# Turning the input with VectorE in blocks of 32 and loading the input projection's weights in four pieces each

## The chip, the cores and the metric

The kernel runs on one core of a Trainium2 chip. Its time is the device time of one execution in microseconds. Three runs before the change took 1353.6, 1354.23 and 1354.41 us (median 1354.23). A profile is one further execution with every engine's instructions recorded. Five engines matter: TensorE (PE; its weight loads are shown as PEld), VectorE (DVE), ScalarE (ACT), GpSimd (POOL) and SyncE (SP), which here only issues transfers. ACT and POOL issue transfers as well.

## The reference, cut to what matters

One step of an encoder layer for two groups of rows that share the weights: 256 new frames of a prompt and 32 frames of a running stream, 288 rows in all, 2048 features each, all in float32.

```
xn   = rmsnorm(x, norm_mix_pre)
proj = xn @ w_in        # 2048 x 5664: [u_pool 1024 | z 2048 | xBC 2560 | dt 32]
pool = trailing-mean pooling mixer on u_pool
ssd  = Mamba-2 mixer on xBC, dt, gated by z   (conv, exact chunked scan, norm)
x    = x + rmsnorm(concat[pool, ssd] @ w_out, norm_mix_post)
up   = rmsnorm(x, norm_ffn_pre) @ w_up        # 2048 x 11264
f    = (silu(conv(gate)) * conv(val)) @ w_down
x    = x + rmsnorm(f, norm_ffn_post)
```

The outputs are the new x of both groups and the new states (pooling rows, two convolution histories, the scan's state).

## The kernel before, in words

**Layout.** Activations are kept transposed: the 128 partitions hold features and the 288 rows lie along the free side. 2048 features are 16 column tiles (KD). A product has 128x128 weights as the stationary operand and 128x288 activations as the moving one, and accumulates over the 16 tiles of features in a PSUM tile `acc` (five buffers).

**Precision.** Each operand is split into a high part, written by ScalarE as float32r, and the rest, subtracted by VectorE. A product is then three matmuls (`mm3`: high x high, high x rest, rest x high). Weights arrive as `raw` (four buffers of up to 1 MB), `split_w` makes `whi` on ScalarE (L146) and `wlo` on VectorE (L147), each with four buffers. The activations' split is `split_from` (L120, L121), which also multiplies by the norm's gain, a value per partition. The row factor of the norm, `rstd`, is applied to the products when VectorE takes them out of PSUM (`conv_in`, `gate_in`, `pool_in`).

**The opening.** `input_tiles` loads x with its rows on the partitions, a chunk of columns at a time. For every column tile TensorE transposes the two prompt blocks and the sample block into PSUM (L299, L300, L301), `split_from` reads PSUM and makes `xn`, and VectorE copies the tile to `xT` (L304), which ScalarE's queue stores to `xT_d` in memory for the residual sum later. `project` with `first_in` as a hook multiplies the columns of B, C and dt (256, 256 and 32 wide) chunk by chunk: 2, 2, 4, 4 and 4 column tiles, each with three weight loads. The narrow dt columns go through `split_narrow`, which puts high part and rest side by side, so that two matmuls do (L185, L186). Ahead of the last chunk `parameters` transposes the small parameters: `columns` three times (L281) and six transposes of `pf` (L325). ScalarE squares whole rows of x with an accumulated sum (L348, L349); from these sums come `rs` and, by six matmuls against the identity (L355), `rstd` on all partitions. It is 16 x (4 x 3 + 2) = 224 matmuls.

**After it.** `project` runs over groups of 256 columns, each with two loads of 1 MB (K16: eight tiles of features in each) and 96 matmuls: eight groups of x for the scan, eight of z, four of u. Between them stands the scan's work. VectorE turns finished 128x288 tiles in blocks of 32 (`blocks_out`, L206, one staging tile `blocks`), SP stores the four strips to memory (L209, `xs_d`), and SP loads them back with rows on the partitions (`xk`, L535 and L536), beside `gb` (L510) and `h0` (L514). VectorE is in every step of this: weight splits, convolution, evacuation, turns. At the start of the output projection `xT` is loaded back from `xT_d` (L887).

**Order.** Each engine and each issuing queue works through its instructions in order. The order is laid out ahead of time by a planner, from priorities and its own estimate of durations; `tc.high_priority` moves instructions forward, `tc.issue_after` puts one behind another on its engine, and `tc.keep_in_program_order` keeps marked instructions of an engine in the order of the source. A load waits on its queue until its buffer is free, and what stands behind it on that queue waits too.

Of the kernel before, what the change touches and what calls it, by code (L numbers as in the profile page):

```python
# [41 lines left out]
TAIL = NT - P  # L42


@with_exitstack
def body(
# [79 lines left out]
    ahead = [0]  # L126

    def fetch_w(view, kb, nk, c0, nc_):
# [22 lines left out]
    def split_narrow(raw, kb, nk, nc_, after):  # L151

        both = xin.tile([P, nk, 2, nc_], F32R, tag="both", bufs=2, name="both")
        with ExitStack() as order:
            order.enter_context(tc.high_priority(offset=ahead[0]))
            for ins in after:
                order.enter_context(tc.issue_after(ins.ins))
            act.activation(both[:, :, 0, :], raw, AF.Copy)
            dve.tensor_tensor(both[:, :, 1, :], raw, both[:, :, 0, :].bitcast(F32), op=ALU.subtract)
        return [(kb + k, both[:, k, :, :].rearrange("p r c -> p (r c)")) for k in range(nk)]  # L160

    def mm3(out, wh, wl, a, start, stop):
        pe.matmul(out, wh, a[:, 0, :], start=start, stop=False)  # L163
        pe.matmul(out, wh, a[:, 1, :], start=False, stop=False)  # L164
        pe.matmul(out, wl, a[:, 0, :], start=False, stop=stop)  # L165

    def project(view, groups, acts, ksplit, before=None, done=None, spare=(), hold=(), behind=None):
# [7 lines left out]
        for i, (kb, n) in enumerate(ksplit):  # L175
# [5 lines left out]
            for raw, (c0, w) in zip(raws, groups):  # L181
                if w < P:
                    for k, both in split_narrow(raw, kb, n, w, after or ()):
                        o = accs[m0][: 2 * w, :]
                        pe.matmul(o, both, acts[k][:, 0, :], start=k == k_first, stop=False)  # L185
                        pe.matmul(o, both, acts[k][:, 1, :], start=False, stop=k == k_last)  # L186
                    continue
                parts = split_w(raw, kb, n, w, ((after or ()) if m0 else ()) + (hold if i else ()))
# [24 lines left out]

    ident = const.tile([P, P], F32, name="ident")
    make_identity(nc, ident)
    ones = const.tile([P, P], F32, name="ones")
    pool.memset(ones, 1.0)
# [7 lines left out]
    tc.keep_in_program_order(act.activation(warm, eps_t, AF.Copy))  # L225
# [22 lines left out]
    start = ExitStack()  # L248
    xin = start.enter_context(tc.tile_pool(name="xin", bufs=1))

    g0_in = xin.tile([KD, P], F32, name="g0_in")
    act.dma_start(out=g0_in, in_=rows(norm_mix_pre))
# [5 lines left out]
    xt = xin.tile([P, 2, D_MODEL], F32, name="xt")  # L258
    xs_ = xin.tile([NS, D_MODEL], F32, name="xs_")
    xpv = x_prompt.rearrange("o (b p) d -> p (o b) d", p=P)  # L260
# [17 lines left out]
    def columns(src, n, name):  # L278
        o = const.tile([P, n], F32, name=name)
        p_ = aux([P, n], "pt")  # L280
        pe.transpose(p_, src, ident[:n, :n])  # L281
        dve.tensor_copy(o, p_)
        return o

    g_mix_pre = columns(g0_in, KD, "g0")


    xn = []
    xT = xin.tile([P, KD, NT], F32, name="xT")
    xT_d = dram.tile([P, KD, NT], F32, name="xT_d")  # L290

    def input_tiles(kb, n):
        c = slice(kb * P, (kb + n) * P)
        sp.dma_start(out=xt[:, :, c], in_=xpv[:, :, c])
        sp.dma_start(out=xs_[:, c], in_=x_sample[0][:, c])
        for t in range(kb, kb + n):
            p_ = aux([P, NT], "pt")
            c = slice(t * P, (t + 1) * P)
            pe.transpose(p_[:, 0:P], xt[:, 0, c], ident)  # L299
            pe.transpose(p_[:, P:NP_], xt[:, 1, c], ident)  # L300
            pe.transpose(p_[:, NP_:NT], xs_[:, c], ident[:NS, :NS])  # L301
# [5 lines left out]
        return last  # L307

    def parameters():
        pb = columns(pb_in, 108, "pb")  # L310
        g_mix_post = pb[:, 60:76]
        g_ffn_pre = pb[:, 76:92]
        g_ffn_post = pb[:, 92:108]
        pa = columns(pa_in, 124, "pa")
        pah = const.tile([P, 100], F32, name="pah")
        act.activation(pah, pa[:, 0:100], AF.Copy, scale=0.5)
        p_scale = pa[:, 100:108]
        g_ssd = const.tile([P, NX], F32, name="g_ssd")
        act.activation(g_ssd, pa[:, 108:124], AF.Copy, scale=0.5)
        pc = columns(pc_in, 120, "pc")  # L320
        pf = const.tile([P, 6, NF * 2], F32, name="pf")
        for i in range(0, 6, 3):
            p_ = aux([P, 3, NF * 2], "ptf")
            for j in range(3):
                pe.transpose(p_[:, j, :], pf_in[:, i + j, :], ident[: NF * 2, : NF * 2])  # L325
            dve.tensor_copy(pf[:, i : i + 3, :], p_)
        return pb, pah, g_mix_post, g_ffn_pre, g_ffn_post, pa, p_scale, g_ssd, pc, pf

    prm = []

    def first_in(kb, n):
        if kb == 12:
            prm.extend(parameters())
        return input_tiles(kb, n)

    win = w_in.rearrange("o (k p) c -> p (o k) c", p=P)
    O_Z, O_X = D_POOL, D_POOL + D_SSD
    O_B, O_C, O_DT = O_X + D_SSD, O_X + D_SSD + 256, O_X + CONV
    first = project(
        win, [(O_B, 256), (O_C, 256), (O_DT, HEADS)], xn, [(0, 2), (2, 2), (4, 4), (8, 4), (12, 4)], first_in  # L340
    )

    ahead[0] = 200
    ssum = xin.tile([P, 3], F32, name="ssum")
    pool.memset(ssum, 1.0)
    junk = xin.tile([P, D_MODEL], F32, name="junk")
    for b in range(2):
        act.activation(junk, xt[:, b, :], AF.Square, accum_out=ssum[:, b : b + 1])  # L348
    act.activation(junk[:NS, :], xs_, AF.Square, accum_out=ssum[:NS, 2:3])  # L349
    rs = xin.tile([P, 3], F32, name="rs")  # L350
    act.activation(rs, ssum, AF.Sqrt, bias=eps_t, scale=1.0 / D_MODEL)
    dve.reciprocal(rs, rs)
    p_ = aux([P, NT], "prs")
    for b, (o, n) in enumerate(BLK):
        pe.matmul(  # L355
            p_[:, o : o + n], rs[:n, b : b + 1].broadcast_to([n, P]), ident[:n, :n], start=True, stop=True
        )
    rstd = const.tile([P, NT], F32, tag="spread", bufs=3, name="rstd")
    dve.tensor_copy(rstd, p_)

    pb, pah, g_mix_post, g_ffn_pre, g_ffn_post, pa, p_scale, g_ssd, pc, pf = prm
    start.close()


# [857 lines left out]
```

## Time and profile before

| what | before |
|---|---|
| median of three runs | 1354.23 us |
| the profiled execution, its own time | 1354.27 us |
| span of its instructions | 1352.6 us |
| TensorE busy | 1340.1 us, 99% |
| VectorE busy | 886.6 us, 66% |
| ScalarE busy | 669.5 us, 50% |
| DMA engines, share on the SP queue | 59.0% |
| granted TensorE clock | 0.999 |
| moved in all | 252.13 MB, mean 186 GB/s |

How to read it: "busy" counts the time in which an engine has an instruction in work; matmuls overlap, so the starts of two matmuls lie closer together than each one's duration (0.29 us). A line such as L163 is a line of the kernel's source. An arrow "out<-in" names the tile written and the tiles read. "x40" is a count. "Idle before" is the engine's pause ahead of an instruction and what ended it. The DMA share is the mean busy share of the core's 16 DMA engines; since packets overlap a little it can go over 1. "To landing" is the time from a transfer's issue to its completion.

### The profile page before, as it was taken

To read this page: it belongs to the slowest core of one execution; us is meant where nothing else is said; L and a number is where in the kernel's file an instruction comes from. 1 tells how busy PE (TensorE), PEld (TensorE's weight loads), DVE (VectorE), ACT (ScalarE), POOL (GpSimd) and SP (SyncE) were. 2 spreads that over 40 slices of the span, in tenths; PEclk is the share of its full clock that TensorE was granted. 3 is DMA by queue.
4 is the path that set the end of the run, shared out by engine and by line. 5 is a ranking of instruction groups with operands and counts; after the bars stand their busy time and mean duration, and the time that the engine had idled before them with its cause. 6 is when DMAs were issued, how large, how long until landed. Compare 5 with 4: busy or idle time off the path is not lost.

```text
span 1352.6 us, 25723 instructions
## 1 busy us (share of the span) xinstructions
PE 1340.1 (99%) x10199; PEld 1327.7 (98%) x10199; DVE 886.6 (66%) x1519; ACT 669.5 (50%) x1003; POOL 233.2 (17%) x394
## 2 busy tenths in 40 slices
PE   8999999999999999999999999999999999999997
PEld 7999999999999999999999999999999999999997
DVE  6898988779644479977676644335666666664454
ACT  6557767446534455645444433334444444454443
POOL 3132112222223320211121100001111111101110
PEclk9999999999999999999999999999999999999999
DMA  8869985464756546876545545554554554576663
GB/s 269 250 192 280 257 249 167 154 221 151 243 179 201 159 132 191 239 196 182 183 156 163 173 144 169 172 179 156 175 168 156 175 169 156 170 232 181 191 182 94
DMA packets 300135, 252.13 MB, mean 186 GB/s; under 512 B 75728, under 2 KB 293050, under 8 KB 299886
## 3 DMA queue, kind: packets, MB, share of 16 engines
q1 hardware_dynamic: 296942, 243.46, 59.0%
q0 software_dynamic: 2320, 4.65, 1.2%
q10 hardware_dynamic: 752, 2.37, 0.5%
q8 instruction: 80, 1.31, 0.4%
q14 instruction: 41, 0.34, 0.1%
HBM read 236.13 MB, written 14.31 MB: 185 GB/s over the span
## 4 chain that ended last, share of the span: by engine, by line
PE 99%; DVE 0%; DMA 0%; ACT 0%; issue 0%; DVEq 0%
PE acc L163 31%; PE acc L165 31%; PE acc L164 31%; PE pst L852 1%; PE py L562 1%; PE acc L1128 1%; PE acc_x L164 0%; PE acc_x L163 0%; PE acc_x L165 0%; PE py L564 0%; DMA xt<-in_x_prompt 0%; PE pt L299 0%; PE acc L1129 0%; PE pt L301 0%; DVE wlo L147 0%; PE acc L186 0%
## 5 line engine op out<-in xcount | busy, mean ns | idle before, releaser
L147 DVE TENSOR_TENSOR wlo<-raw,whi 128x1024 fp32r<-128x1024 f32 (+1 forms) x416 | 493.3, 1188 | 347.9 <-ACT whi L146 346.6
L146 ACT ACTIVATE whi<-raw 128x1024 fp32r<-128x1024 f32 (+1 forms) x416 | 426.6, 1028 | 498.0 <-PE acc L164 421.0
L163 PE MATMUL acc<-hn,whi 128*128 128x288 f32 x1376 | 404.1, 295 | 0.0
L164 PE MATMUL acc<-hn,whi 128*128 128x288 f32 x1376 | 403.6, 294 | 0.3 <-DVE hn L911 0.3
L165 PE MATMUL acc<-hn,wlo 128*128 128x288 f32 x1376 | 403.1, 294 | 0.0
L164 PEld LDWEIGHTS acc<-hn,whi 128*128 128x128 f32 x1376 | 259.7, 189 | 0.7 <-DVE hn L911 0.7
L165 PEld LDWEIGHTS acc<-hn,wlo 128*128 128x128 f32 x1376 | 259.6, 189 | 0.0
L163 PEld LDWEIGHTS acc<-hn,whi 128*128 128x128 f32 x1376 | 257.2, 187 | 0.1
L163 PE MATMUL acc<-xn,whi 128*128 128x288 f32 x704 | 209.3, 299 | 0.0
L164 PE MATMUL acc<-xn,whi 128*128 128x288 f32 x704 | 208.0, 296 | 0.0
L165 PE MATMUL acc<-xn,wlo 128*128 128x288 f32 x704 | 207.2, 296 | 0.0
L163 PE MATMUL acc<-fa,whi 128*128 128x288 f32 x682 | 201.9, 296 | 0.0
L164 PE MATMUL acc<-fa,whi 128*128 128x288 f32 x682 | 201.9, 296 | 0.0
L165 PE MATMUL acc<-fa,wlo 128*128 128x288 f32 x682 | 201.5, 295 | 0.0
L164 PEld LDWEIGHTS acc<-xn,whi 128*128 128x128 f32 x704 | 133.6, 190 | 0.3
L165 PEld LDWEIGHTS acc<-xn,wlo 128*128 128x128 f32 x704 | 132.9, 189 | 0.3
L163 PEld LDWEIGHTS acc<-xn,whi 128*128 128x128 f32 x704 | 132.4, 189 | 0.5
L164 PEld LDWEIGHTS acc<-fa,whi 128*128 128x128 f32 x682 | 128.6, 188 | 0.0
L163 PEld LDWEIGHTS acc<-fa,whi 128*128 128x128 f32 x682 | 128.1, 188 | 0.0
L165 PEld LDWEIGHTS acc<-fa,wlo 128*128 128x128 f32 x682 | 127.9, 188 | 0.0
L945 POOL COPY fc_stage<-ebuf 128x4 f32<-128x4 f32 x88 | 27.8, 316 | 503.6 <-DVE ebuf L944 460.2
L951 DVE SCALAR_TENSOR_TENSOR fc<-ebuf,pf,fc 128x290 f32<-128x290 f32 x176 | 90.4, 517 | 3.1 <-ACT fc L949 0.5
(341 smaller groups left out, 1660.7 us busy)
## 6 DMA issues: line engine op xcount, KB each, us to landing
raw<-in_w_up SPq DMA_DIRECT2D x80, 1024.0 KB, 5.2
raw<-in_w_in SPq DMA_DIRECT2D x40, 1024.0 KB, 5.7
raw<-in_w_down SPq DMA_DIRECT2D x32, 1024.0 KB, 5.3
raw<-in_w_out SPq DMA_DIRECT2D x24, 1024.0 KB, 5.6
raw<-in_w_down SPq DMA_DIRECT2D x16, 768.0 KB, 5.0
raw<-in_w_up SPq DMA_DIRECT2D x14, 512.0 KB, 4.1
gb<-g_d SPq DMA_DIRECT2D x8, 832.0 KB, 5.4
raw<-in_w_in SPq DMA_DIRECT2D x6, 512.0 KB, 6.0
```

Of the source, the lines that this page charges most:

```text
L146: act.activation(hi, raw[:, k : k + n, :], AF.Copy)
L147: dve.tensor_tensor(lo, raw[:, k : k + n, :], hi.bitcast(F32), op=ALU.subtract)
L163: pe.matmul(out, wh, a[:, 0, :], start=start, stop=False)
L164: pe.matmul(out, wh, a[:, 1, :], start=False, stop=False)
L165: pe.matmul(out, wl, a[:, 0, :], start=False, stop=stop)
L562: ins = pe.matmul(y[c, 0:256], xw[:, 0, f_], m[:, h, 0:256], start=True, stop=False)
L852: ins = pe.matmul(st[:, o, :], x_, btok[:, gi, b, :], start=b != 1, stop=b != 0)
L945: pool.tensor_copy(fc_stage[:, :, :, i], e[:, 256:324].rearrange("p (s c) -> p s c", c=34)[:, :, 0:2])
L951: dve.scalar_tensor_tensor(c, e[:, r_ : r_ + 290], pf[:, r_, i : i + 1], c, op0=ALU.mult, op1=ALU.add)
L1128: pin(pe.matmul(o, hi, f2[k][:, :, c], start=k == 0, stop=end, skip_group_check=True))
```

## The change: what it does

**Layout of the features.** A tile of 128 features is no longer 128 neighbouring columns. Tile k now has, on the partitions 32i to 32i+31, the columns 512i + 32k to 512i + 32k + 31, for i from 0 to 3. x is loaded so that the partitions 32i to 32i+31 hold 32 rows, with the columns from 512i on, and the nine blocks of 32 rows lie along the free side (`xt`, 128 x 9 x 4 x 128). A VectorE transpose in blocks of 32x32 (`turn_x`) then makes the tile `xT[k]` directly in SBUF. `turn_x(i + 1)` stands ahead of the splits of chunk i.

**Loads.** Each piece of x (16 of the prompt, 8 of the sample) and each weight load of the input projection now comes as four transfers, by 32 partitions. For the opening, a weight chunk has B, C and dt side by side (544 columns). There are nine chunks: one, one, and then two tiles each. The order of all these loads is fixed in the source.

**The rest of the opening.** Everything in it is kept in program order. TensorE runs 17 matmuls on a constant tile first. ScalarE takes the squares in nine slices, three in each of three chunks, and copies the transposed parameters (VectorE did). The row sums are spread to all partitions by one matmul over `spots`. The 16 tiles `xT` are stored to `xT_d` by SP after the opening, and loaded back in 16 pieces that put the features into their natural order.

```diff
+NB = 512
+CHUNKS = ((0, 1), (1, 1), (2, 2), (4, 2), (6, 2), (8, 2), (10, 2), (12, 2), (14, 2))
+BUSY = 17
...
     def fetch_w(view, kb, nk, c0, nc_):
         raw = wpool.tile([P, nk, nc_], F32, tag="raw", name="raw")
         with tc.high_priority(offset=ahead[0]):
-            sp.dma_start(out=raw, in_=view[:, kb : kb + nk, c0 : c0 + nc_])
+            if len(view.shape) == 4:
+                for i in range(4):
+                    sp.dma_start(
+                        out=raw[NS * i : NS * (i + 1)], in_=view[i, :, kb : kb + nk, c0 : c0 + nc_]
+                    )
+            else:
+                sp.dma_start(out=raw, in_=view[:, kb : kb + nk, c0 : c0 + nc_])
         return raw
...
+    busy = xin.tile([P, NT], F32R, name="busy")
+    for o, n in BLK:
+        pin(dve.tensor_copy(busy[:, o : o + n], ones[:, 0:n]))
...
+    xt = xin.tile([P, 9, 4, P], F32, name="xt")
+    xpv = x_prompt.rearrange("o (b t) (i c w) -> i t (o b) c w", t=NS, i=4, w=P)
+    xsv = x_sample.rearrange("o t (i c w) -> i (o t) c w", i=4, w=P)
+    win = w_in.rearrange("o (i k f) w -> i f (o k) w", i=4, f=32)
...
+    for i in range(4):
+        input_load(sp, 0, i)
+    sample_load(act, slice(0, 1))
+    first_load(*CHUNKS[0], (act, act, sp, sp))
+    for kb, n in CHUNKS[1:3]:
+        first_load(kb, n)
+    for c in range(1, 4):
+        for i in range(4):
+            input_load(sp, c, i)
+        if c == 1:
+            sample_load(sp, slice(1, 4))
+            first_load(*CHUNKS[3])
...
-            pe.transpose(p_[:, 0:P], xt[:, 0, c], ident)
-            pe.transpose(p_[:, P:NP_], xt[:, 1, c], ident)
-            pe.transpose(p_[:, NP_:NT], xs_[:, c], ident[:NS, :NS])
-            a = atile("xn")
-            last = split_from(a, p_, g_mix_pre[:, t : t + 1])
-            dve.tensor_copy(xT[:, t, :], p_)
-            xn.append(a)
-        act.dma_start(out=xT_d[:, kb : kb + n, :], in_=xT[:, kb : kb + n, :])
...
+    keep_busy(BUSY - 4)
     g_mix_pre = columns(g0_in, KD, "g0")
+    keep_busy(4)
...
+    def turn_x(i):
+        for t in range(CHUNKS[i][0], sum(CHUNKS[i])) if i < len(CHUNKS) else ():
+            xT.append(btile("xT"))
+            pin(dve.transpose(
+                xT[t].rearrange("p (b t) -> p b t", t=NS), xt[:, :, t // 4, 32 * (t % 4) : 32 * (t % 4 + 1)]
+            ))
+
+    def prepare(i):
+        kb, n = CHUNKS[i]
+        raw = raws.pop(0)
+        w = xin.tile([P, n, 2 * NB + 3 * HEADS], F32R, tag="w", bufs=4, name="w")
+        hi, lo = w[:, :, : NB + HEADS], w[:, :, NB + HEADS : 2 * (NB + HEADS)]
+        tiles = range(kb, kb + n)
+        turn_x(i + 1)
+        if i == 0:
+            pin(act.activation(hi, raw, AF.Copy))
+        for t in tiles:
+            if t >= len(xn):
+                xn.append(atile("xn"))
+            pin(act.activation(xn[t][:, 0, :], xT[t], AF.Copy, scale=g_mix_pre[:, t : t + 1]))
+        if i:
+            pin(act.activation(hi, raw, AF.Copy))
+        pin(act.activation(w[:, :, 2 * (NB + HEADS) :], raw[:, :, NB:], AF.Copy))
+        for t in tiles:
+            pin(dve.scalar_tensor_tensor(
+                xn[t][:, 1, :], xT[t], g_mix_pre[:, t : t + 1], xn[t][:, 0, :].bitcast(F32),
+                op0=ALU.mult, op1=ALU.subtract,
+            ))
+        last_split[:] = [pin(dve.tensor_tensor(lo, raw, hi.bitcast(F32), op=ALU.subtract))]
+        if i + 4 < len(CHUNKS):
+            first_load(*CHUNKS[i + 4])
+        for b in range(3 * (i - 4), 3 * (i - 3)) if 4 <= i < 7 else ():
+            pin(act.activation(junk, xt[:, b].rearrange("p c w -> p (c w)"), AF.Square, accum_out=ssum[:, b : b + 1]))
+        if i == 6:
+            pool.tensor_tensor(
+                spots, ssum.unsqueeze(2).broadcast_to([P, 9, NS]), sel4.unsqueeze(1).broadcast_to([P, 9, NS]), op=ALU.mult
+            )
+        return w
...
+    turn_x(0)
+    ahead_w = [prepare(0)]
+    for i, (kb, n) in enumerate(CHUNKS):
+        if i + 1 < len(CHUNKS):
+            ahead_w.append(prepare(i + 1))
+        if i == 4:
+            pb = columns(pb_in, 108, "pb", copies)
+            pa = columns(pa_in, 124, "pa", copies)
+            pc = columns(pc_in, 120, "pc", copies)
+        if i == 5:
+            for q in range(0, 6, 3):
+                p_ = aux([P, 3, NF * 2], "ptf")
+                for j in range(3):
+                    pin(pe.transpose(p_[:, j, :], pf_in[:, q + j, :], ident[: NF * 2, : NF * 2]))
+                copies.append((pf[:, q : q + 3, :], p_))
+        for o, p_ in copies:
+            pin(act.activation(o, p_, AF.Copy))
+        copies.clear()
+        if i == 6:
+            p_ = aux([P, NT], "prs")
+            pin(pe.matmul(p_, ones, spots.rearrange("p b t -> p (b t)"), start=True, stop=True))
+            rstd = const.tile([P, NT], F32, tag="spread", bufs=3, name="rstd")
+            pin(act.activation(rstd, p_, AF.Sqrt, bias=eps_t, scale=1.0 / D_MODEL))
+            pin(dve.reciprocal(rstd, rstd))
...
-    xs_ps = [project(win, [(O_X, 256)], xn, K16)]
+    xs_ps = [project(win, [(O_X, 256)], xn, K16, wait=last_split)]
+    for t in range(KD):
+        pin(sp.dma_start(out=xT_d[t], in_=xT[t]))
...
-            sp.dma_start(out=xT, in_=xT_d)
+            for j in range(4):
+                for i in range(4):
+                    sp.dma_start(
+                        out=xT[NS * j : NS * (j + 1), 4 * i : 4 * (i + 1), :],
+                        in_=xT_d.rearrange("(q j) (i f) n -> j i f q n", j=4, i=4)[j, i],
+                    )
```

More of the change, by code (lines that the diff above doesn't have):

```diff
@@ L149, in split_w, with mm3, project @@
         return out
[L151 to L167, printed above, removed]
+    def mm3(out, wh, wl, a, start, stop, then=lambda ins: ins):
+        then(pe.matmul(out, wh, a[:, 0, :], start=start, stop=False))
+        then(pe.matmul(out, wh, a[:, 1, :], start=False, stop=False))
+        then(pe.matmul(out, wl, a[:, 0, :], start=False, stop=stop))
+    def project(view, groups, acts, ksplit, before=None, done=None, spare=(), hold=(), behind=None, wait=()):
         n_all = sum(-(-w // P) for _, w in groups)
@@ L181, in project @@
             for raw, (c0, w) in zip(raws, groups):
[L182 to L188, printed above, removed]
+                parts = split_w(raw, kb, n, w, tuple(wait) + ((after or ()) if m0 else ()) + (hold if i else ()))
                 for q, part in enumerate(parts):
```

148 lines of the change are left out of this document (76 added, 72 removed).

## The prediction

> **What bounds the kernel now.** I read the page's first part and the chain that ended last, then the busy time by stretches, then the opening instruction by instruction, and last the transfers.
>
> ```profile
> ## 1 busy us (share of the span) xinstructions
> PE 1340.1 (99%) x10199; PEld 1327.7 (98%) x10199; DVE 886.6 (66%) x1519; ACT 669.5 (50%) x1003; POOL 233.2 (17%) x394
> ...
> PE 99%; DVE 0%; DMA 0%; ACT 0%; issue 0%; DVEq 0%
> ```
>
> TensorE is the bound all the way, so the change can win only where TensorE does something other than products at full pace, and lose wherever it makes TensorE wait. That place is the opening (each stretch: length, then busy time and instructions per engine, clock, DMA share, GB/s):
>
> ```profile
> 0.00:7.27 7.27, 2.03 (x9) 1.52 (x10) 3.62 (x7) 3.00 (x5) 6.63 (x42) 1.00 0.63 178
> 7.27:12.33 5.06, 5.06 (x22) 4.63 (x21) 4.07 (x10) 2.30 (x5) 2.97 (x6) 1.00 0.99 324
> 12.33:52.40 40.07, 40.07 (x288) 37.36 (x287) 26.69 (x55) 25.17 (x39) 6.39 (x12) 1.00 0.89 274
> ```
>
> The first product with a weight starts at 7.27. Until 12.33 products come 0.24 us apart, later 0.132 us. Up to 64.6 us the trace has 344 of them, 45.4 us at 0.132, so 19.2 us of the opening are not products at full pace: 7.2 before the first, 3.0 of slow pace, 9.0 of other TensorE work up to 52.4. From 52.4 to 100 that sum stays at 19.1 to 19.3, so 19.2 us is all that can be won. Most of the 9.0 is the input's transposes:
>
> ```profile
> 20.24 0.29 PE L163 MATMUL acc<-xn,whi 128*128 128x288 f32 x1
> 20.37 0.27 PE L299 MATMUL pt<-ident,xt 128*128 128x128 f32 x1
> 20.48 0.27 PE L300 MATMUL pt<-ident,xt 128*128 128x128 f32 x1
> 20.68 0.24 PE L301 MATMUL pt<-ident,xs__137 32*128 32x32 f32 x1
> 20.86 0.41 PE L164 MATMUL acc<-xn,whi 128*128 128x288 f32 x1
> 21.10 0.27 PE L299 MATMUL pt<-ident,xt 128*128 128x128 f32 x1
> ```
>
> A column tile costs 20.37 to 20.86 and 0.11 us of the product behind it: 0.6 us, 13 times after 12.33, 7.8 us.
>
> Then the transfers. In the last stage three 64 KB loads into 32 partitions each (xr_s, issued 1197.1 to 1198.5) go between two large weight loads; their packets run from 1201 to 1204.7. The other lines are the input projection:
>
> ```profile
> 1200.00:1201.00 1.00, 1.00 (x11) 0.99 (x10) 0.96 (x4) 0.65 (x1) 0.00 (x0) 1.00 1.09 348
> 1202.00:1204.50 2.50, 2.50 (x21) 2.50 (x20) 1.94 (x5) 0.97 (x3) 0.00 (x0) 1.00 1.11 240
> 60.00:100.00 40.00, 40.00 (x304) 40.00 (x303) 37.75 (x81) 19.44 (x27) 11.63 (x12) 1.00 0.71 190
> 100.00:200.00 100.00, 100.00 (x815) 96.93 (x814) 91.16 (x185) 73.72 (x146) 17.03 (x22) 1.00 0.89 262
> 200.00:330.00 130.00, 130.00 (x1046) 127.79 (x1045) 103.35 (x180) 73.95 (x125) 26.42 (x35) 1.00 0.58 180
> ```
>
> With the narrow loads in the rings the DMA share stays full but the rate falls from 348 to 240 GB/s. Between 100 and 200 us the DMA share is 0.89 and VectorE is 91% busy: little room there.
>
> **The change, part by part.**
>
> *TensorE.* Removed: 48 input transposes and, of the six matmuls of rstd, all but one. The nine parameter transposes stay (1.3 us). The 17 filler matmuls run before the first product, where TensorE is idle; they cost nothing unless the first product is early, and then 0.24 us each.
>
> *VectorE.* 16 copies out of PSUM (0.45 us) become 16 block transposes of the same 128x288 (L206: 0.47), a wash in sum. But the transposes of chunk i+1 now stand ahead of the splits of chunk i. What queues behind one that waits for its input are the splits of a chunk whose weights have long landed, and TensorE behind those.
>
> *First transfers.* x is 24 pieces instead of 10 loads, the first weights 36 pieces instead of 15 loads. SP issues one in 0.48 us (L294, L295, L131). Before tiles 4 and 5 can be turned, SP has issued 22 pieces: 0.83 + 22 x 0.48 = 11.4 us, 2.4 us on to landing (as g_in, 2.5), 13.8.
>
> *Pace of the narrow pieces.* No row has a load made of narrow pieces alone. Ends: 350 GB/s, as whole loads; and 184 GB/s, the lowest slices of the stretch 1200 to 1206. I take 240, the only row with such pieces.
>
> *Chain of the opening at 240 GB/s*, with start-to-start times (ACT: weights 1.03, x 0.43; VectorE: turn 0.40, x 0.45, weights 1.22; chunk of two tiles on TensorE 28 x 0.132 = 3.7). First weights land 7.2, first product 8.2; the two one-tile chunks at 0.24 run to 14.9. Tiles 4 and 5 turned at 14.6, chunk 2 split at 16.7, its products end 20.1; chunk 3 ends 23.8. Chunk 4's weights are behind all of x: 4.6 MB, 24.6; split 26.8, products, with the parameter transposes ahead of them, end 30.3. Now ACT binds. Squares come in nine slices of 512 (L146 at 128x512 is 0.63, plus 0.09 for the accumulator: 0.64 net), three behind each of chunks 4 to 6, and the parameter copies, VectorE's before, stand behind the second three. The pf transposes need the PSUM slots those copies free: TensorE waits 2.0, chunk 5 ends 36.5. The rstd matmul waits for the last squares 0.8, chunk 6 ends 41.3, chunks 7 and 8 48.7 (the table load of Sqrt, 1.28, hides under chunk 6). Less 224 products (29.6) that is 19.1 us lost against 19.2: **no gain in the opening**. At 350 GB/s the same chain ends at 46.1 (gain 2.6), at 184 at 54.6 (loss 5.8).
>
> *xT store and reload.* Five stores from ACT become 16 on SP, one reload (288.5) becomes 16: 7.2 us of SP each at 0.45. A weight load is issued when VectorE frees one of four buffers (SP's longest wait is for L147, 670 us in 142 waits), some 3 x 6.34 = 19 us ahead of need, and lands in 5.7: 13 us of cover. Cost zero; if the cover is gone, up to 7 each.
>
> *40 weight loads of 1 MB in four pieces.* 120 more issues, 54 us of SP over 300 us in which it mostly waits: no cost. A megabyte takes 1024 x 52 ns / 16 = 3.3 us now and 4.4 at 240 GB/s. From 100 to 200 us there are 15.5 of them: share 0.89 + 0.17 = 1.06, which is full (rows reach 1.04 to 1.11 when saturated). TensorE is not starved by that alone. But queues lengthen, and the stores of xs_d stand in them: they land in 4.4 us (up to 8.9), and VectorE, with one staging tile, already waits 11.0 us for them. Of the 15 spacings between its block transposes 11 are under 9 us; with landings 2 us longer, half of those 22 us reach VectorE: 11 us, with 8.8 idle in that stretch. The split tiles ahead of TensorE (four of 3.2 us) take most; I put 4 us on TensorE. Ends: zero, and 18 at 184 GB/s (below).
>
> [...]
>
> Sum: profiled execution 1354.3 (span 1352.6 and 1.7 around it; the median is 1354.2) - 0.1 + 4 = **1358**.
>
> **The rivals.**
>
> *Faster.* Pieces following one another in the rings mix, since the 16 engines run up to 3 us apart (the xr_s packets are spread over 3.7 us), and a load goes at the old 330 to 350. For it: packets of other loads are back at 50 ns at once. Then the opening gains 2.6 and up to 6 if ACT and the first landings do better than charged (ACT's two waits, 2.8), and nothing is lost later: 1348 to 1352, say 1350. Against it: the 240 row.
>
> *Hidden.* Half pace, but both queues of slack hold: 1354, 1352 to 1357. That the four loads are hidden and the opening a wash.
>
> *Much slower.* The pieces go at 184 GB/s: 5.7 us per megabyte, share 0.89 + 0.37 = 1.26 from 100 to 200, that is 18 us over a full 1.08, less 10 of cover, and the opening's 5.8: 1368 to 1374. It decides from about 4.6 us per megabyte on. Against it: in those slices other stores ran too.
>
> **How the numbers follow.** Forecast (1357 to 1364) 0.36, faster 0.34, hidden 0.18, much slower 0.12. A measurement here tells 0.2%, 2.7 us, from nothing: faster below 1351.5, slower over 1356.9. Slower: most of the first (0.33), the last (0.12), a little of hidden: 0.46. Faster 0.33, same 0.21. The range leaves out the fastest and slowest tenth: 1348 to 1371; the likeliest's own is 1355 to 1364.
>
> **What would show it.** Right: VectorE idle ahead of the turn of tile 4 until about 13 to 14 us; TensorE waiting ahead of the pf transposes and the rstd matmul; the last first-stage product near 48 us; DMA share over 1 and under 280 GB/s between 100 and 200; longer landings of xs_d, and TensorE idle after 60 us. Wrong: weight pieces landing at 330 GB/s, a first stage done before 45, TensorE without gaps after 60 us.

## The result: 2.8% slower

The changed kernel takes 1392.3 us (median of 4 runs, 1391.28 to 1392.94) against 1353.97 us for the kernel before on the same chip: 1.0282 times, 95% interval 1.0264 to 1.03, so 38.3 us more. The forecast was 1358, its range 1348 to 1371. The profiled execution spans 1390.1 us. The same two parts of the page as before, busy time and the chain that ended last by engine:

```profile
PE 1347.1 (97%) x10164; PEld 1333.8 (96%) x10164; DVE 886.9 (64%) x1511; ACT 670.3 (48%) x1023; POOL 236.6 (17%) x394
...
PE 84%; DMA 10%; SPq 2%; DVE 1%; ACT 1%; issue 1%; DVEq 0%
PE acc L162 27%; PE acc L164 27%; PE acc L163 27%; DMA raw<-in_w_in 4%; DMA xs_d<-blocks 2%; DMA gb<-g_d 1%; DMA xk<-xs_d 1%; PE pst L934 1%; SPq L137 1%; DMA xt<-in_x_prompt 1%; PE acc L1215 1%; DVE wlo L157 1%; DMA xT_d<-xT 1%; DMA xt<-in_x_sample 0%; DMA h<-in_state_ssd 0%
```

TensorE was the whole chain before; now a tenth of the span hangs on transfers. By stretches (length, busy time and instructions per engine, granted clock, DMA share, GB/s):

```profile
0.00:8.48 8.48, 4.50 (x19) 3.96 (x19) 3.59 (x11) 2.62 (x6) 7.84 (x44) 1.00 0.66 154
8.48:18.72 10.24, 5.80 (x29) 5.36 (x29) 2.92 (x6) 3.49 (x8) 3.92 (x7) 0.83 1.04 217
18.72:30.00 11.28, 8.96 (x49) 8.64 (x50) 8.04 (x15) 5.11 (x11) 0.00 (x0) 0.70 1.13 219
30.00:40.00 10.00, 9.22 (x73) 8.78 (x71) 7.20 (x13) 9.41 (x27) 0.56 (x4) 1.00 1.03 218
40.00:46.00 6.00, 0.35 (x2) 0.22 (x2) 0.01 (x1) 3.64 (x8) 0.67 (x1) 0.75 1.15 203
46.00:59.60 13.60, 13.47 (x86) 12.90 (x86) 10.56 (x11) 7.19 (x11) 0.00 (x0) 0.86 1.07 282
60.00:100.00 40.00, 36.99 (x266) 36.79 (x267) 31.06 (x71) 17.23 (x26) 12.44 (x14) 0.96 0.97 165
100.00:200.00 100.00, 90.20 (x698) 86.68 (x696) 77.34 (x166) 60.43 (x120) 18.59 (x24) 0.95 0.99 215
200.00:330.00 130.00, 124.66 (x999) 121.03 (x1000) 98.64 (x149) 72.19 (x122) 25.55 (x31) 0.99 0.91 180
```

Two things are to be seen. From 8.5 to 46 us the DMA engines are full (share 1.03 to 1.15) at 203 to 219 GB/s, where the kernel before, between 7.3 and 12.3 us, moved 324 at a share of 0.99. And from 60 to 330 us, where the kernel before kept TensorE busy all the time, TensorE now has 18.2 us without work (3.0, 9.8 and 5.3), with the DMA share at 0.97, 0.99 and 0.91 instead of 0.71, 0.89 and 0.58. TensorE's waits up to 62 us and from 62 to 330 us, two answers one after the other (line, what it waited for: us in total, times, longest):

```profile
PE acc L420 <- DVE xn L369: 5.7, 1, 5.7
PE prs L409 <- POOL spots L380: 5.7, 1, 5.7
PE acc L420 <- ACT xn L364: 2.3, 1, 2.3
...
PE ptf L402 <- ACT pb L405: 0.8, 1, 0.8
```
```profile
PE acc L164 <- DVE wlo L157: 10.4, 7, 4.3
PE py L644 <- DVE m L632: 5.0, 1, 5.0
PE ptok L544 <- DVE g L527: 2.5, 1, 2.5
```

Where the time was lost can be followed by TensorE's work: the start of the n-th matmul that accumulates into `acc`, in both kernels (every trace has 9704 of them). The lag of the changed kernel behind the one before is 11.5 us when the opening's 224 products are done (48.8 us before), 11.6 at 64 us, 16.1 at 70, 17.3 at 100, 37.6 at 206, and the same from there on. So about a third is lost in the opening, 6 us where the opening meets the first large loads, 20 us between 100 and 206, and nothing after. (Taken at the moment when VectorE takes a product out of PSUM, the lag is 9.0 us at the opening's `v`, at 52.4 us before, and 20.3 at the first group of x, at 63.3; those moments shift with VectorE's order too, so "lag" below is by products.)

### The profile page after: what moved, and what is told of

Read it like the earlier page. It is cut to its first block, busy times and chain, and to the rows that moved or that the text cites. A ratio compares the mean times of both kernels' runs of the same rounds, so it can differ in the third digit from the quotient of the medians.

```text
span 1390.1 us, 25931 instructions
## 1 busy us (share of the span) xinstructions
PE 1347.1 (97%) x10164; PEld 1333.8 (96%) x10164; DVE 886.9 (64%) x1511; ACT 670.3 (48%) x1023; POOL 236.6 (17%) x394
## 4 chain that ended last, share of the span: by engine, by line
PE 84%; DMA 10%; SPq 2%; DVE 1%; ACT 1%; issue 1%; DVEq 0%
PE acc L162 27%; PE acc L164 27%; PE acc L163 27%; DMA raw<-in_w_in 4%; DMA xs_d<-blocks 2%; DMA gb<-g_d 1%; DMA xk<-xs_d 1%; PE pst L934 1%; SPq L137 1%; DMA xt<-in_x_prompt 1%; PE acc L1215 1%; DVE wlo L157 1%; DMA xT_d<-xT 1%; DMA xt<-in_x_sample 0%; DMA h<-in_state_ssd 0%
## 5 line engine op out<-in xcount | busy, mean ns | idle before, releaser
L157 DVE TENSOR_TENSOR wlo<-raw,whi 128x1024 fp32r<-128x1024 f32 (+1 forms) x406 | 482.5, 1191 | 343.4 <-ACT whi L156 342.2
L156 ACT ACTIVATE whi<-raw 128x1024 fp32r<-128x1024 f32 (+1 forms) x406 | 417.2, 1031 | 464.1 <-PE acc L163 389.9
L164 PE MATMUL acc<-xn,wlo 128*128 128x288 f32 x640 | 191.1, 299 | 10.4 <-DVE wlo L157 10.4
L162 PE MATMUL acc<-xn,whi 128*128 128x288 f32 x640 | 192.3, 300 | 0.8 <-DVE ebuf L461 0.8
L163 PE MATMUL acc<-xn,whi 128*128 128x288 f32 x640 | 190.5, 298 | 0.0
L164 PEld LDWEIGHTS acc<-xn,wlo 128*128 128x128 f32 x640 | 122.6, 192 | 12.1 <-DVE wlo L157 12.0
L162 PEld LDWEIGHTS acc<-xn,whi 128*128 128x128 f32 x640 | 121.9, 190 | 1.5 <-PE acc L427 1.1
L163 PEld LDWEIGHTS acc<-xn,whi 128*128 128x128 f32 x640 | 122.9, 192 | 0.2
L1028 POOL COPY ebuf<-pf 128x2 f32<-128x2 f32 x88 | 71.2, 809 | 129.3 <-DVE fc L1039 58.4
```

Of the source, the lines that this page charges most:

```text
L156: act.activation(hi, raw[:, k : k + n, :], AF.Copy)
L157: dve.tensor_tensor(lo, raw[:, k : k + n, :], hi.bitcast(F32), op=ALU.subtract)
L162: then(pe.matmul(out, wh, a[:, 0, :], start=start, stop=False))
L163: then(pe.matmul(out, wh, a[:, 1, :], start=False, stop=False))
L164: then(pe.matmul(out, wl, a[:, 0, :], start=False, stop=stop))
L1028: pool.tensor_copy(e[:, 258:260], pf[:, 4:6, i])
```

## The experiments

Three theories stood after this. **One, pace**: a load that writes 32 neighbouring partitions keeps the DMA engines longer per byte, and everything follows from that. **Two, count**: 120 more loads cost by their number, on SP and in the queues of the DMA engines (the rings). **Three, order**: the opening's new order of instructions is what loses, and what follows is its echo. The time of the kernel before beside each run is between 1353.7 and 1354.3; differences below are of medians on one chip, except where two batches are compared.

### The kernel before, with only the large loads cut

**Four loads by 32 partitions** (`b_strips`). The loads of 1 MB of the input projection are cut as in the change, all else is the kernel before:

```diff
-            sp.dma_start(out=raw, in_=view[:, kb : kb + nk, c0 : c0 + nc_])
+            for i in range(4):
+                q = slice(NS * i, NS * (i + 1))
+                sp.dma_start(out=raw[q], in_=view[q, kb : kb + nk, c0 : c0 + nc_])
```

> The kernel before, with one edit: each of the 40 one-megabyte weight loads of the input projection after the opening is issued as four loads of 32 partitions each. Theory 1 (a load that writes 32 partitions goes at about 215 GB/s, and the transfers are then full from 60 to 215 us): 12 to 30 us slower than before, 1366 to 1384 us, DMA share near 1 and under 240 GB/s between 100 and 200 us. Theory 2 (four times as many issues on SP): the same loss here and in the cut by rows. Theory 3 (the loss of the changed kernel is all in its opening and the order it leaves behind): within 3 us of before.

The diff, like the next three, does not show the test that picks these 40 loads. Measured: 1380.65 us (1379.18 to 1383.07), 1.02 times (1.0185 to 1.0215), 26.9 us more. The stretches from 60 us on:

```profile
60.00:100.00 40.00, 37.09 (x278) 36.63 (x277) 31.22 (x69) 16.71 (x23) 12.47 (x12) 1.00 1.06 186
100.00:200.00 100.00, 89.15 (x710) 84.91 (x709) 76.54 (x158) 60.00 (x118) 17.13 (x21) 0.98 0.99 217
200.00:330.00 130.00, 125.44 (x984) 122.23 (x983) 103.58 (x170) 72.09 (x124) 29.96 (x35) 0.97 0.94 189
```

They are nearly the changed kernel's own: 217 GB/s at a share of 0.99, and 10.9 us of TensorE without work between 100 and 200. The opening of this kernel is the old one (lag -0.6 us after 224 products), so theory three cannot be the whole.

**Four loads by feature tiles** (`b_rows`): as many loads and the same 1-KB packets, but each writes all 128 partitions.

```diff
-            sp.dma_start(out=raw, in_=view[:, kb : kb + nk, c0 : c0 + nc_])
+            for i in range(0, nk, 2):
+                sp.dma_start(out=raw[:, i : i + 2, :], in_=view[:, kb + i : kb + i + 2, c0 : c0 + nc_])
```

> The kernel before, with the same 40 loads issued as four loads each, but cut along the rows: 128 partitions by two tiles of features, 256 KB each, the same number of issues and the same packets as the cut by partitions. Theory 1: within 3 us of before (1351 to 1357). Theory 2: as slow as the cut by partitions, 1366 to 1384.

Measured: 1355.82 us (1353.94 to 1359.21), 1.0016 (1.0006 to 1.0026). The number of loads costs 2.1 us, not 27: theory two falls.

**Two loads by 64 partitions** (`b_halves`), against `b_strips`:

```diff
-            for i in range(4):
-                q = slice(NS * i, NS * (i + 1))
+            for i in range(2):
+                q = slice(2 * NS * i, 2 * NS * (i + 1))
```

> The kernel before, with the same 40 loads issued as two loads each, by 64 partitions. [...] Theory 1 in the form that the width counts: about half the loss of four pieces. Theory 2: a third of it (80 issues more instead of 120 gives 40 against 120).

Measured: 1386.61 us (1385.55 to 1387.15), 1.0241 (1.0226 to 1.0257): 32.9 us more, 6.0 more than by 32, with half as many loads. So neither the width of a load nor the number of loads sets the loss, and 64 neighbours are no better than 32.

**Four loads by every fourth partition** (`b_spread`): 32 partitions in each load again, but the load i writes partitions i, i+4, i+8 and so on.

```diff
-                q = slice(NS * i, NS * (i + 1))
+                q = slice(i, P, 4)
```

> The kernel before, with its 40 loads of 1 MB of the input projection's weights (8 feature tiles by 256 columns) issued as four loads each, the load i writing every fourth partition from i on. As many loads, packets of the same 1 KB and the same partitions per load (32) as in the run that cut them by 32 neighbouring partitions, which cost 26.9 us; only which 32 partitions one load writes differs. Theory A, that the pace hangs on how many partitions one load writes: about the same cost, 1376 to 1385 us. [...]

Measured: 1356.16 us (1355.16 to 1357.24), 1.0015 (1.0006 to 1.0024). Either the pace hangs on how many partitions a load writes (A), or on where they lie. A falls: at 2.1 us more than before, 32 partitions are not slow as such. It matters which 32. Stretch 100 to 200 us of `b_halves`, of `b_rows` and of `b_spread`:

```profile
100.00:200.00 100.00, 87.79 (x670) 83.72 (x669) 74.47 (x155) 59.73 (x117) 16.64 (x21) 0.93 0.97 209
```
```profile
100.00:200.00 100.00, 99.66 (x811) 96.36 (x810) 88.38 (x178) 71.56 (x141) 17.95 (x22) 1.00 0.91 257
```
```profile
100.00:200.00 100.00, 97.19 (x789) 93.65 (x788) 87.42 (x179) 71.03 (x141) 16.51 (x22) 1.00 0.87 247
```

The records of single packets say the same. Mean time that a 1-KB packet held its DMA engine, of those started between 100 and 200 us, by what one load writes:

```
before    128 partitions, 8 tiles               53 ns
b_rows    128 partitions, 2 tiles               55 ns
b_spread  32 partitions, every fourth           55 ns
b_strips  32 neighbouring partitions            79 ns
b_halves  64 neighbouring partitions            82 ns
after     32 neighbouring partitions            82 ns
```

16 engines at 1 KB in 82 ns are 200 GB/s; at 53 ns 309.

Such a cut also changes which rows of the weights a load reads together. That does not decide the pace: one load of the changed kernel reads 256 neighbouring rows, one of `b_strips` eight groups of 32, and both go at about 80 ns; the whole loads of the kernel before and those of `v_act` below read different rows too, 1024 and 512 neighbours, at 53 ns both.

### The changed kernel, with whole large loads

`a_whole` is the change with each load of 1 MB in one piece again; its rows do not fit the features, so its products are of the wrong pairs.

```diff
-                for i in range(4):
-                    sp.dma_start(
-                        out=raw[NS * i : NS * (i + 1)], in_=view[i, :, kb : kb + nk, c0 : c0 + nc_]
-                    )
+                view = w_in.rearrange("o (k p) c -> p (o k) c", p=P)
+            sp.dma_start(out=raw, in_=view[:, kb : kb + nk, c0 : c0 + nc_])
```

> The changed kernel, with the 40 one-megabyte loads of the input projection after the opening as single loads of 128 partitions again, of neighbouring rows of the weights (those rows do not belong to the features that the activations hold, so the products are of the wrong pairs; the work is the same). Theory 1: of the 38 us the part after the opening goes, 18 to 29 us, and the opening's 9 to 20 us stay: 1363 to 1375 us. Theory 3: 1385 us or more.

Measured: 1366.95 us (1366.15 to 1368.77), 1.0099 (1.0084 to 1.0114). 25.4 us of the 38.3 are gone (25.1 by each one's own runs of the kernel before); the 13.2 that stay belong to the rest of the change. After 60 us:

```profile
60.00:100.00 40.00, 40.00 (x305) 40.00 (x304) 36.84 (x81) 19.95 (x30) 17.33 (x12) 1.00 0.74 200
100.00:200.00 100.00, 97.12 (x780) 93.83 (x780) 84.38 (x175) 67.17 (x137) 18.59 (x23) 0.98 0.81 240
200.00:330.00 130.00, 129.68 (x1039) 127.04 (x1038) 103.74 (x172) 71.56 (x116) 29.10 (x36) 1.00 0.65 186
```

Its lag in the profile is 9.4 us when the opening's products are done, 9.5 still at 100 us and 14.9 at 206: most of what stays is lost in the opening, and 5.4 us between 100 and 206, with the DMA share at 0.81. Taken away here (25.4) or added there (26.9), the pieces of the large loads cost the same, so this part of the account does not hang on the opening.

### The opening

TensorE's second wait in the changed kernel, 5.7 us ahead of the product with rstd's sums, has no transfer in its name. ScalarE shows whom it waited for (start, us, engine, line; idle before and its releaser):

```profile
42.36 2.00 ACT L156 ACTIVATE whi<-raw 128x1024 fp32r<-128x1024 f32 x2 [2.86 <-DMA raw<-in_w_in]
44.27 0.61 ACT L377 ACTIVATE junk<-xt 128x512 f32<-128x512 f32 x1
```

The ninth square (L377) stands behind two splits of the first ordinary weights, which nothing but the planner's choice had put there, and these waited for their load. `a_act` ties those splits to the last weight copy of the last chunk on ScalarE:

```diff
-        pin(act.activation(w[:, :, 2 * (NB + HEADS) :], raw[:, :, NB:], AF.Copy))
+        tail = pin(act.activation(w[:, :, 2 * (NB + HEADS) :], raw[:, :, NB:], AF.Copy))
...
-        last_split[:] = [pin(dve.tensor_tensor(lo, raw, hi.bitcast(F32), op=ALU.subtract))]
+        last_split[:] = [pin(dve.tensor_tensor(lo, raw, hi.bitcast(F32), op=ALU.subtract)), tail]
```

> The changed kernel with one more order: the splits of the first ordinary weight tiles on ScalarE (whi, line 156) wait for the last weight copy of the last chunk on ScalarE as well as for VectorE's last split, so that they cannot stand ahead of the squares. In the changed kernel two of them waited 2.86 us for their load ahead of the third square of chunk 6, and the product with rstd's sums then waited 5.7 us on TensorE. Theory A: that wait is a loss of its own; the time falls by 3 to 6 us, to 1386 to 1389. Theory B: the join behind the opening waits for raw, xT_d and h over the busy queue anyway, so what the opening gains is waited for there: 1390 to 1393.

Measured: 1388.69 us (1387.09 to 1389.35), 1.0254 (1.0239 to 1.0269): 3.6 us less. TensorE's wait and its busy time behind the opening:

```profile
PE prs L409 <- POOL spots L380: 0.9, 1, 0.9
```
```profile
40.00:50.00 10.00, 9.33 (x69) 9.22 (x70) 7.98 (x9) 9.97 (x16) 0.62 (x1) 1.00 1.09 246
50.00:60.00 10.00, 9.18 (x69) 8.93 (x69) 9.72 (x23) 4.67 (x10) 2.07 (x7) 1.00 1.13 243
60.00:80.00 20.00, 15.29 (x108) 15.06 (x107) 10.09 (x23) 6.52 (x8) 0.49 (x2) 0.93 0.97 188
```

The lag at the end of the opening falls from 11.5 to 4.5 us, so this order was most of it. But between 60 and 80 us TensorE is idle for 4.7 us now, where the changed kernel's had 3.0, and the lag is 15.8 at 100 us, where it was 17.3: part of the gain is waited away behind the same full rings. Both theories were right in part.

### Other features, so that every weight load is whole

The turn in blocks of 32 asks only that partition 32i+f of a tile holds a feature that lies in the i-th group of partitions of the loaded input. With tile 4c+k holding feature 512c+4p+k on partition p, a weight load reads rows that lie evenly apart and can write all 128 partitions, and VectorE turns every fourth column. `v_whole`:

```diff
-    xpv = x_prompt.rearrange("o (b t) (i c w) -> i t (o b) c w", t=NS, i=4, w=P)
+    xpv = x_prompt.rearrange("o (b t) (c i w) -> i t (o b) c w", t=NS, i=4, w=P)
...
-    win = w_in.rearrange("o (i k f) w -> i f (o k) w", i=4, f=32)
+    win = w_in.rearrange("o (c p k) w -> p (o c) k w", p=P, k=4)
...
-                xT[t].rearrange("p (b t) -> p b t", t=NS), xt[:, :, t // 4, 32 * (t % 4) : 32 * (t % 4 + 1)]
+                xT[t].rearrange("p (b t) -> p b t", t=NS), xt[:, :, t // 4, t % 4 :: 4]
...
```

> The changed kernel with another assignment of features: tile 4c+k has feature 512c+4p+k on partition p, so that every weight load of the input projection, the opening's too, writes all 128 partitions (a 1-MB load is two loads of 512 KB); VectorE turns columns four apart; the input still comes in pieces of 32 partitions with its 512-byte runs; the gains come as a column without TensorE's transpose; the copy of the input in HBM is stored and read back without pieces. Theory A, that only loads that write a quarter of the partitions are slow: the 25 us of the projection's loads come back as with whole loads of the wrong features (1367), and the opening's 4.46 MB of weights at some 330 instead of 220 GB/s return some 6 to 7 us more: 1358 to 1363, still slower than before by the input's pieces. Theory B, that the opening is held by VectorE and ScalarE's order and not by its weights: 1365 to 1369.

Measured: 1363.53 us (1363.43 to 1363.93), 1.0071 (1.0054 to 1.0088). The 25 us are back with the right products, and 3.4 us more against `a_whole` (3.8 by each one's own runs of the kernel before) for the opening's weights, the gains and the input's copy together. The time lies between the two ranges, half a microsecond above theory A's. In the profiles the lag at the end of the opening falls from 9.4 (`a_whole`) to 4.4 us, 5.0 of the 6 to 7 that theory A gave to the opening's weights; of that 3.4 to 3.8 are left in the time (the profiled execution of `a_whole` was itself 1.8 us over its median).

`v_act` adds the order of `a_act` to it:

> The kernel with all weight loads on 128 partitions, and the order on ScalarE besides (the first ordinary splits behind the last weight copy of the last chunk). Theory A: 2 to 5 us under the kernel without that order, some 1354 to 1360, about the time before or a little over. Theory B: no change against it (within 1.5 us), since with faster loads the splits no longer wait ahead of the squares.

Measured: 1360.23 us (1359.75 to 1362.8), 1.0049 (1.0034 to 1.0064), 3.3 us less: theory A. It is the fastest form of the change that was run, and still 6.2 us over the kernel before. Its lag is 2.6 us at the end of the opening, 2.7 still at 120 us and 6.5 at 206. From 10 to 20 us, by halves, it still goes

```profile
10.00:15.00 5.00, 5.00 (x24) 4.74 (x22) 1.61 (x3) 2.33 (x4) 2.24 (x5) 1.00 1.01 181
15.00:20.00 5.00, 1.27 (x5) 0.95 (x5) 4.00 (x7) 2.29 (x5) 0.69 (x1) 0.76 1.15 223
```

at 181 and 223 GB/s: the input is still written by 32 partitions.

### The input

`v_blocks` is `v_act` with the input cut by blocks of 32 tokens, so that each load writes all 128 partitions:

```diff
-    def input_load(queue, c, i):
-        pin(queue.dma_start(out=xt[NS * i : NS * (i + 1), 0:8, c, :], in_=xpv[i][:, :, c, :]))
+    def input_load(queue, c, b):
+        v = xpv[:, :, b, c, :] if b < 8 else xsv[:, :, 0, c, :]
+        pin(queue.dma_start(out=xt[:, b, c, :], in_=v))
```

> The kernel with whole weight loads and the order on ScalarE (1360.2), with the input cut by blocks of 32 tokens instead of by partitions: each load takes 32 tokens by four times 128 features and writes all 128 partitions, nine loads for each group of four tiles instead of eight, packets of the same 512 bytes. If only the partitions that one load reaches set the pace, the input's 2.36 MB go at some 330 instead of some 200 GB/s, the turn of tiles 4 and 5 comes 3 to 4 us sooner, and with the opening's 8 us of waits on TensorE a part of that reaches the end: 1354 to 1358. If the pace of the input hangs on its 512-byte runs, 1359 to 1362.

Measured: 1377.42 us (1375.98 to 1377.83), 1.0169 (1.0154 to 1.0184): 17 us worse than `v_act`, where a gain was expected. The pace did what was expected: the input's 512-byte packets took 29 ns in the mean instead of 46 (started between 2 and 35 us). What was not foreseen is how long SP takes to issue such a load: 0.53 to 1.75 us, median 0.72. The chain of the opening (start, us, what):

```profile
5.21 9.26 DMA raw<-in_w_in
14.48 0.78 SPq L228
15.31 0.73 SPq L228
16.08 0.73 SPq L228
16.85 1.32 SPq L228
18.21 0.79 SPq L233
...
34.09 0.72 SPq L228
34.95 5.60 DMA raw<-in_w_in
```

L228 is the load of a block of the input, L233 that of the opening's weights. From 14.5 us on SP issues with hardly a pause until 34.8 us, and the last chunks' weights stand behind. A piece by 32 partitions, twice as large, is issued in 0.45 us (L231 of the changed kernel, in the chain of its opening). So the chain went from the rings to SP's queue; ahead of that it has a weight load that took 9.26 us to land, and why is not shown. The DMA share from 25 to 40 us is 0.29 and 0.58:

```profile
25.00:30.00 5.00, 3.78 (x14) 3.46 (x15) 4.99 (x8) 2.53 (x5) 0.00 (x0) 0.50 0.29 83
30.00:40.00 10.00, 6.48 (x46) 6.25 (x44) 2.10 (x4) 0.00 (x0) 0.00 (x0) 0.94 0.58 161
```

`v_stores` takes `v_blocks` and issues the 16 stores of the turned input in the opening instead of behind it:

```diff
-    for t in range(KD):
-        pin(sp.dma_start(out=xT_d[t // 4, :, t % 4, :], in_=xT[t]))
...
+        for t in {5: range(0, 6), 6: range(6, 12), 7: range(12, 16)}.get(i, ()):
+            pin(sp.dma_start(out=xT_d[t // 4, :, t % 4, :], in_=xT[t]))
```

> The kernel with the input by blocks, with the 16 stores of the turned input issued during the last three chunks of the opening (some 30 to 40 us, where the transfers' share was 0.63) instead of between the weights of the join. If those 2.36 MB between the loads of the join are what is left of the loss behind the opening (+6 us between 100 and 230 us), 3 to 6 us less than without, 1349 to 1354, at or under the time before; if the loss there comes from the weights' two loads for one or from the later order on VectorE, no change within 2 us.

Measured: 1378.28 us (1375.76 to 1380.27), 1.0182 (1.0165 to 1.0199), no change. It does not settle much: the opening of this kernel ends some 15 us later than that of `v_act`, so the room that the stores were to use was not where it had been.

`v_queues` is `v_act` with the pieces of the lower 64 partitions issued by SP and those of the upper 64, with the last tokens, by ScalarE:

```diff
-        input_load(sp, 0, i)
+        input_load((sp, sp, act, act)[i], 0, i)
-    sample_load(act, slice(0, 1))
-    first_load(*CHUNKS[0], (act, act, sp, sp))
+    sample_load(act, slice(0, 1))
+    first_load(*CHUNKS[0])
...
-            input_load(sp, c, i)
+            input_load((sp, sp, act, act)[i], c, i)
-            sample_load(sp, slice(1, 4))
+            sample_load(act, slice(1, 4))
```

> The kernel with whole weight loads and the order on ScalarE (1360.2), the input again in pieces of 32 partitions, but those of the lower 64 partitions issued by SyncE and those of the upper 64 with the last tokens by ScalarE, so that both halves can be written at once; every weight load of the opening is SyncE's. [...] If the pace hangs on each packet by itself (154 ns for 2 KB in a narrow load whatever else runs), the rate stays and the time is 1359 to 1363.

Measured: 1363.03 us (1362.27 to 1363.71), 1.0067 (1.0052 to 1.0082). The input's packets took 45 ns in the mean, as on one queue (46); two queues to two halves do not give the pace back, and the stretch from 10 to 25 us went at 246, 191 and 148 GB/s in its three parts of 5 us, where `v_act` had 181, 223 and 243. ScalarE, with 17 loads to issue ahead of its splits, was late besides:

```profile
PE acc L416 <- ACT xn L360: 14.7, 1, 14.7
```

`v_eights` is `v_queues` in groups of eight tiles (feature 1024c+8p+k), so that a megabyte is one load again and the input's runs are 1 KB:

```diff
...
-    win = w_in.rearrange("o (c p k) w -> p (o c) k w", p=P, k=4)
+    win = w_in.rearrange("o (c p k) w -> p (o c) k w", p=P, k=8)
...
-                xT[t].rearrange("p (b t) -> p b t", t=NS), xt[:, :, t // 4, t % 4 :: 4]
+                xT[t].rearrange("p (b t) -> p b t", t=NS), xt[:, :, t // 8, t % 8 :: 8]
...
```

> The kernel of v_queues with groups of eight feature tiles instead of four: tile 8c+k has feature 1024c+8p+k on partition p, so that each 1-MB load of the projection is one load again, the input's runs are 1 KB and its pieces half as many, and VectorE turns columns eight apart. The split of each 1-MB load in two cost about 2 us by the runs that cut it in four (2.1 and 2.1 us): 2 us less by that. The first tile waits for 1.18 MB of the input instead of 0.59, some 2 to 3 us later, which the later chunks can make up only if the opening is not held by its transfers. 1353 to 1357 if they do, 1357 to 1362 if they don't.

Measured: 1362.48 us (1359.74 to 1364.6), 1.0069 (1.0052 to 1.0085), not to be told from `v_queues`. None of these forms beats the kernel before.

## Why the prediction was wrong

**The step that failed is the pace of the narrow pieces, and with it the 4 us put on TensorE for the 40 weight loads.** The runs give 26.9 us for them alone (`b_strips`) and 25.4 in place (`a_whole`). The mechanism was in the text, in the rings, in VectorE and in the third rival; the sizes were off. The other large miss is the opening, put at nothing and measured at 11.5 us of lag (below).

- *The pace.* 240 GB/s came from a stretch in which three narrow loads lay among others. Where nearly all loads are such pieces, in the changed kernel's opening, the rows show 203 to 219, and between 100 and 200 us a 1-KB packet takes 82 ns: a megabyte takes 1024 x 82 / 16 = 5.2 us, not 4.4. A rate of mixed traffic was taken for a rate of one kind.
- *What full means.* A share of 1.06 was called bearable, because short rows reach 1.04 to 1.11. Over 100 us the rings of `b_strips` held 0.99 (over the 40 us before, 1.06, at only 186 GB/s). The kernel before moved 26.2 MB between 100 and 200 us, by its 262 GB/s; at the 217 GB/s of `b_strips` that takes 121 us, 21 more. The lag of `b_strips` grows by 21.0 us from 100 to 206 us (4.0 to 25.0). So the stretch was bound by its transfers, and the 8.8 us of VectorE's idle time and the split tiles did not cover it.
- *Where it counts.* Only 100 to 200 us was costed. `b_strips` is level with the kernel before at 64 us and 4.0 us behind at 100, after the first large loads: about a sixth of the loss lies ahead of the stretch that was reckoned.

The way it reaches TensorE was foreseen: the landings of xs_d went from 4.4 us (median) to 5.8, two microseconds having been put, and VectorE's waits for them rose by 14.6 us from 62 to 330 us, where 11 had been reckoned from 100 to 200. Of before and of after:

```profile
DVE blocks L206 <- DMA xs_d<-blocks: 11.0, 4, 4.4
```
```profile
DVE blocks L199 <- DMA xs_d<-blocks: 25.6, 10, 4.9
DVE wlo L157 <- ACT whi L156: 15.7, 14, 2.0
DVE h0t L601 <- DMA h<-in_state_ssd: 8.7, 1, 8.7
DVE xw L621 <- DMA xk<-xs_d: 7.0, 4, 2.8
```

What it left out is that the other loads of the scan, h and xk, wait in the same rings.

**The opening was not a wash.** The first terms held: weights at 7.34 us (7.2 put), first product at 8.48 (8.2). Of the 22 pieces that tiles 4 and 5 need, SP issued the last four, of the sample, from 10.94 us on, and was done at 12.9 us, not 11.4:

```profile
10.94 2.00 SPq L228 DMA_DIRECT2D xt<-in_x_sample  x4
```

The last of them landed at 18.3 us, 5.7 us after its issue had begun, not 2.4. The 2.4 was the landing of a load in nearly empty rings. So the turn came at 18.72 instead of 14.6, and chunk 4's weights were split from 28.04 on (landing put at 24.6). The idle VectorE is there as described, but until 18.7 us instead of 13 to 14:

```profile
18.72 0.84 DVE L346 STREAM_TRANSPOSE xT<-xt 128x288 f32<-128x288 f32 x2 [7.33 <-DMA raw<-in_w_in]
```

The pf transposes waited 0.8 us (2.0 put). The rstd matmul waited 5.7 (0.8 put), and not for the squares' own time: the count of ScalarE's work left out that the planner may put splits of the next stage into it. The first stage ended at 59.6 us instead of 48.7. One more size: in stretches in which TensorE waits, or just behind them, the granted clock is lower, 0.70 between 18.7 and 30 us and 0.86 between 46 and 59.6, and the 0.132 us per product of the chain was not to be had there.

**What held.** The 120 more issues cost 2.1 us (`b_rows`, `b_spread`), near the nothing that was put. That the opening gives no gain nearly held, but only for `v_act`, without the slow weight loads and with the other order on ScalarE: its opening ends 2.6 us behind the old one. In the change itself it lost 11.5 us, twice the 5.8 of the pessimistic end. The xT stores' zero was not separated: they lie on the chain of the opening's end (an xT_d landing from 52.4 to 59.4 us), and the one run that moved them had another bound.

**The rivals.** "Faster" rested on pieces in the rings mixing back to 330 to 350 GB/s; no stretch shows that. "Hidden" fails with TensorE's idle time after 60 us. "Much slower", given 0.12, was the case: its point of decision, 4.6 us per megabyte, is passed by the 5.2 measured. Its price of 1368 to 1374 was too low although its pace was too slow (5.7), because it let the share reach 1.08, took 10 us of cover that was not there, and counted nothing before 100 us. What the runs show is that which partitions one load writes decides, and not how many: 32 neighbours and 64 go at 79 and 82 ns per packet, all 128 at 53, and 32 of them, every fourth, nearly at the pace of all 128 (55 ns). A second queue, for the upper 64 partitions, does not help (`v_queues`, 45 ns against 46). Why neighbours are slow was not shown.

**What stays open.** The 6.2 us of `v_act` are not explained. By its lag 2.6 us are lost in the opening, where the input's pieces still are, and nearly 4 between 120 and 206 us, with the DMA share at 0.84 and 0.58 in the rows of 100 to 200 and 200 to 300 us. TensorE's only listed wait there, from 85 to 235 us, is for VectorE's weight split:

```profile
PE acc L164 <- DVE wlo L157: 2.8, 3, 1.6
```

Whether that comes from the megabyte in two loads (cutting it in four cost 2.1 us in the kernel before) or from the later stages' other order was not separated.

## What to carry to other kernels

Before cutting a load, look at which partitions each piece writes: pieces by neighbouring partitions, 32 or 64, made packets take one and a half times as long (79 and 82 ns against 53) and cost 26.9 and 32.9 us, while pieces by rows, or by every fourth partition (55 ns both), cost 2.1 us each. If a layout asks for blocks of 32, choose the assignment of features so that the large operand still loads whole, and let the small one be cut. And cost a slower transfer by the bytes of the whole stretch at the rate measured with such loads (26.2 MB at 217 GB/s gave the 21 us that were seen), not by the share that a saturated row reaches.

## What the runs showed that was not expected

- 64 neighbouring partitions in one load are no faster than 32: 82 against 79 ns per KB, and the kernel 6.0 us slower with half as many loads.
- 32 partitions, every fourth, go at 55 ns per KB, whole loads at 53.
- A load of 64 KB over 128 partitions from 512-byte runs was issued in 0.72 us by SP (median), one of 128 KB over 32 partitions in 0.45: the better pace in the rings came with 17 us lost, and SP's issues on the chain.
- 7.0 us won at the end of the opening (`a_act`) came out as 3.6 at the end of the kernel, while its transfers stayed full.
